# Order of weight and conditioning loads, unbroken conditioning visits and a run of ten output products in a hybrid decoder block

## The chip, the core and the metric

The kernel runs on one core of one Trainium2 chip. The metric is the device time of one execution in microseconds (us). The kernel before takes 1383.16 us, the median of three runs (1382.48 to 1385.14).

A core has five engines that run their own instruction streams: TensorE (PE) does matrix products, with the loads of its stationary operand listed apart as PEld; VectorE (DVE), ScalarE (ACT) and GpSimd (POOL) work on elements; SyncE (SP) issues DMAs here. Sixteen DMA engines move data between main memory and the core. Each engine takes its instructions in the order of its own stream, so an instruction that waits holds up all that stands behind it on that engine.

## What is computed

One layer of a decoder for two groups of tokens: 256 tokens of a prompt and 8 x 4 tokens of samples, 288 columns in all, with a model width of 2048. Cut to what matters:

```python
mod = silu(c) @ w_ada + b_ada                 # 6 parts of 2048 per conditioning vector
sh1, sc1, g1, sh2, sc2, g2 = split(mod, 6)
h = rmsnorm(x, norm1) * (1 + sc1) + sh1
u_pool, z, xbc, dt_raw = split(h @ w_in)      # 512, 1536, 2560, 24 columns
pool_out = pool_mixer(u_pool)
ssd_out  = ssd_mixer(z, xbc, dt_raw)          # conv, 24 heads x 64, state 128, chunks of 128
x = x + g1 * (concat(pool_out, ssd_out) @ w_out)
h2 = rmsnorm(x, norm2) * (1 + sc2) + sh2
gate, val = split(h2 @ w_up)                  # 2 x 5504
x = x + g2 * ((silu(causal_conv(gate)) * val) @ w_down)
y = rmsnorm(x, norm_f)
```

All is float32. `c` has nine rows: one for the prompt, eight for the samples. "Conditioning" below means the product of silu(c) with the 2048 x 12288 matrix `w_ada`.

## The kernel before, in words

**Layout.** Activations lie with features on the 128 partitions and the 288 tokens along the free axis; the width of 2048 is 16 feature tiles (KT). A large product is done as three matmuls in a reduced float32 format (`mm3`, L224 to L228): the weight tile is split into a high part (a cast on ScalarE, L220) and a low part (a subtraction on VectorE, L221), the activation likewise (h1h, h1l; L368, L369), and high x high, high x low and low x high are summed in PSUM. Each weight comes from main memory in loads of 512 KB (`load`, L210 to L213), issued by the sync queue in the order of its stream, into a ring of "raw" slots: 16 during the first stage, 8 after it, 9 from the output projection on.

**Order.** The code is written as generators that yield after a unit of work, and `pull(gen, rate)` (L871) runs another generator by so many units. What is written earlier has the higher priority; a planner then fills each engine's stream, taking of the instructions that its model holds to be ready the one with the highest priority. `tc.high_priority()` raises an instruction above the rest, and `tc.keep_in_program_order` keeps it behind the instruction written last on that engine. The order on each engine is fixed when the program is built.

**First stage.** The input projection cannot start before the first norm is modulated, and the modulation needs two parts (shift and scale) of the conditioning. Both are therefore cut by feature tiles into six groups, `KGROUPS`, of 1, 1, 2, 4, 4 and 4 tiles. `ada_group_units(gi)` (L275) loads the `w_ada` columns of a group (4, 4, 8, 16, 16, 16 loads), multiplies them in visits of four loads (records "adag", L303), transposes the result ("adat_g"), and `modulate` (L352) makes h1h and h1l of the group. `xbc_units(gi)` (L554) then multiplies the group's rows of `w_in` for 28 column tiles (a unit is one column tile; in groups 0 and 1 one load holds eight units) and adds the result to what the groups before gave: group 0 is copied from PSUM by ScalarE (L574), the others are added by VectorE (L576). The generator `nxt` runs the conditioning of groups 1 to 5 and their modulation. Its first five units come ahead of the products of group 0, and during group `gi` it is pulled at `AN[gi+1] / (ET - 4)` per unit, with ET = 28.

**Second stage.** With group 5 come the convolution, the state space mixer (`ssd_group`, L634), the pooling mixer and the remaining columns of `w_in` (records "mm_uz"), all interleaved (`back`). In `ssd_group`, `decays(t)` makes for two heads the decay factors e (all tokens) and ec (second chunk), with the last step of both on VectorE; `outputs(t)` (L725) sums ten products of 64 columns for the two heads into one PSUM bank: yo with a selection matrix, and xdt of each chunk with e, and s1 (the state after the first chunk) with ec. Each float32 product appears as two records in the trace.

**Later conditioning.** Four further parts of the conditioning are not needed at once. `ada_part_units(part, ay)` (L329) goes through the 16 feature tiles: two loads and four products each with 32 output rows in a column strip of their own (`ada_mm`, L252; records "adap", L255). Parts 2, 3 and 4 run with AY = 2, so a unit, or "visit", is two feature tiles: four loads, eight products, 16 records. They are pulled a fraction of a visit at a time during the second stage and the output projection (`adas`). Part 5 runs with `ay` = 1 during the first pairs of the gated MLP.

**Then** follow the output projection ("mm_out"), the up projection in pairs of gate and value ("mm_gate", "mm_val"), interleaved with the down projection in three groups ("mm_down"), and the last norm.

Of the kernel before, what the change touches and what calls it, by code (L numbers as in the profile page):

```python
# [17 lines left out]
P = 128  # L18
D = 2048
KT = D // P  # L20
NP = 256
NB, NL = 8, 4
NS = NB * NL
N = NP + NS
# [11 lines left out]
ET = XT + len(UEARLY) + 3 * ZEARLY  # L36
# [4 lines left out]
YK = 2  # L41
AQ = (4, 4, 4, 4, 4, 4)

AN = (5, 5, 7, 11, 14, 15)
AY = 2

RA1, RA2, RB1, RB2, RB3 = 0.5, 0.4, 1.0, 1.0, 1.0
# [86 lines left out]
def kernel(ctx: ExitStack, tc, ins, outs):  # L134
    nc = tc.nc
# [8 lines left out]
    def aux(name):  # L144
        return px.tile([P, 512], F32, tag="aux", name=name)
# [11 lines left out]
    seli = vec[:, K_SEL:K_SEL + 32]  # L157
# [9 lines left out]
    sc_c = kp.tile([P, KT, 32], F32, name="sc_c")  # L167
# [42 lines left out]
    def load(key):  # L210
        off, cols = S.items[key]
        t = wp[0].tile([P, RAWC], F32, tag="raw", name="raw_" + "_".join(map(str, key)))
        nc.sync.dma_start(t[:, :cols], wflat[off:off + P * cols].rearrange("(p n) -> p n", p=P))  # L213
        return t

    def split(raw, a, n, name, urgent=True):
        hi = wp[0].tile([P, RAWC], F32R, tag="whi", name="whi_" + name)
        lo = wp[0].tile([P, RAWC], F32R, tag="wlo", name="wlo_" + name)
        with tc.high_priority() if urgent else nullcontext():
            nc.scalar.copy(hi[:, :n], raw[:, a:a + n])  # L220
            nc.vector.tensor_tensor(lo[:, :n], raw[:, a:a + n], hi[:, :n].bitcast(F32), ALU.subtract)  # L221
        return hi, lo

    def mm3(ps, whi, wlo, c, bh, bl, first, last, n=P):  # L224
        w = slice(c * n, c * n + n)
        nc.tensor.matmul(ps, whi[:, w], bh, start=first, stop=False)  # L226
        nc.tensor.matmul(ps, whi[:, w], bl, start=False, stop=False)  # L227
        nc.tensor.matmul(ps, wlo[:, w], bh, start=False, stop=last)  # L228

    ready = {}  # L230
# [21 lines left out]
    def ada_mm(ps, raw, k, c0, nb, js):  # L252
        for j in js:
            c = c0 + (j - js[0]) * nb
            nc.tensor.matmul(ps[32 * j:32 * j + 32, :nb], sc_c[:, k, :], raw[:, c:c + nb],  # L255
                             start=(k == 0), stop=(k == KT - 1), tile_position=(0, 32 * j))

    def ada_sb(ps, nb, name, r=P):
        asb = kp.tile([P, 512], F32, tag="asb", name="asb_" + name)
        nc.scalar.copy(asb[0:r, :nb], ps[0:r, :nb])  # L260
        return asb

    def ada_tr(asb, nb, name, r=P):
        pt = aux("adat_" + name)
        for i in range(nb // P):
            nc.tensor.transpose(pt[:, i * r:(i + 1) * r], asb[0:r, i * P:(i + 1) * P], ident[0:r, 0:r])
        return pt

    def ada_scale(which, part, norm, k0, gk):
        nc.vector.scalar_tensor_tensor(  # L270
            out=amul[:, which, k0:k0 + gk, :], in0=ada[:, part, k0:k0 + gk, :], scalar=1.0,
            in1=norm[:, k0:k0 + gk].unsqueeze(2).to_broadcast([P, gk, NC9]),
            op0=ALU.add, op1=ALU.mult)
# [54 lines left out]

    def ada_part_units(part, ay=1):  # L329
        ps = pa.tile([P, 512], F32, tag="ada", name=f"adap{part}")  # L330
        for k in range(KT):
            raws = [load(("adap", part, k, h)) for h in range(2)]
            for h in range(2):
                ada_mm(ps, raws[h], k, 0, 512, range(2 * h, 2 * h + 2))
            if k % ay == ay - 1:
                yield
        asb = ada_sb(ps, 512, f"p{part}")
        yield
        pt = ada_tr(asb, 512, f"p{part}")
        for i in range(4):  # L340
            o = ada[:, part].rearrange("p (j i) c -> p j i c", j=4)[:, :, i, :]
            b = bada[:, part].rearrange("p (j i) -> p j i", j=4)[:, :, i]
            src = pt[:, i * P:(i + 1) * P].rearrange("p (j c) -> p j c", j=4)[:, :, 0:NC9]
            nc.vector.tensor_tensor(o, src, b.unsqueeze(2).to_broadcast([P, 4, NC9]), ALU.add)
        if part == 4:
            ada_scale(1, 4, vec[:, V_N2:V_N2 + KT], 0, KT)
        yield
# [56 lines left out]
    for q in range(4):  # L404
        t = mx.tile([P, 4, N], F32, tag="blk", name=f"xa{q}", bufs=4)
# [11 lines left out]
    for q in range(4):  # L417
# [216 lines left out]
    def ssd_group(g):  # L634
# [10 lines left out]
        xdt = kp.tile([P, 3, G6], F32, tag="hmod", name=f"xdt{g}", bufs=2)  # L645
# [27 lines left out]
        s1 = sx[0].tile([P, G6], F32, tag="s1", name=f"s1_{g}")  # L673
# [18 lines left out]
        for i in range(2):  # L692
            for j in range(4):
# [3 lines left out]
                                 tile_position=(0, 32 * j))  # L697
        yo = sx[0].tile([P, G6], F32, tag="yo", name=f"yo{g}")
# [26 lines left out]
        def outputs(t, e, ec):  # L725
            assert (g, t) in zdone
            pq = aux(f"y{g}_{t}")
            rows = [slice(0, 64), slice(64, P)]
            for i, r in enumerate(rows):
                f = slice(64 * (2 * t + i), 64 * (2 * t + i) + 64)  # L730
                nc.tensor.matmul(pq[r, NP:N], yo[:, f], seli, start=True, stop=False)
            for i, r in enumerate(rows):
                f = slice(64 * (2 * t + i), 64 * (2 * t + i) + 64)
                nc.tensor.matmul(pq[r, NP:N], xdt[:, 2, f], e[:, i, NP:N], start=False, stop=True)
            for i, r in enumerate(rows):
                f = slice(64 * (2 * t + i), 64 * (2 * t + i) + 64)
                nc.tensor.matmul(pq[r, 0:P], xdt[:, 0, f], e[:, i, 0:P], start=True, stop=True)
            for i, r in enumerate(rows):
                f = slice(64 * (2 * t + i), 64 * (2 * t + i) + 64)
                nc.tensor.matmul(pq[r, P:NP], xdt[:, 1, f], e[:, i, P:NP], start=True, stop=False)  # L740
                nc.tensor.matmul(pq[r, P:NP], s1[:, f], ec[:, i, :], start=False, stop=True)
            yt = cf[:, t, 0:N]
            nc.vector.scalar_tensor_tensor(out=yt, in0=yt,
                                           scalar=vec[:, V_D + 3 * g + t:V_D + 3 * g + t + 1],
                                           in1=pq[:, :N], op0=ALU.mult, op1=ALU.add)
            zt = zy[g][:, t, :]
            nc.vector.tensor_tensor(zt, zt, yt, ALU.mult)
            sq = kp.tile([P, N], F32, tag="xsq", name=f"ysq{g}_{t}", bufs=2)
            nc.scalar.activation(sq, zt, AF.Square)
            if g + t == 0:  # L750
                nc.gpsimd.tensor_copy(ssq, sq)
            else:
                nc.gpsimd.tensor_tensor(ssq, ssq, sq, ALU.add)
# [117 lines left out]
    def pull(gn, rate):  # L871

        credit[id(gn)] = credit.get(id(gn), 0.0) + rate
        while credit[id(gn)] >= 1:
            credit[id(gn)] -= 1
            next(gn, None)

    ready["xbc", 0, 0] = load(("xbc", 0, 0))
    for _ in range(AN[0]):
        next(nxt)  # L880
    for gi in range(len(KGROUPS)):
        last = gi + 1 == len(KGROUPS)
        if last:

            wp[0].drop(w0)
            w0_ctx.close()
            sx[0] = mx_ctx.enter_context(tc.tile_pool(name="sx", bufs=1, reuse_waits="tile"))
            hi, lo = split(load(("dt",)), 0, KT * NH, "dt")
            ps = pm.tile([P, 512], F32, tag="mm", name="mm_dt")
            for k in range(KT):  # L890
                mm3(ps[0:NH, :N], hi, lo, k, xhi[0][k], xlo[0][k], k == 0, k == KT - 1, NH)
            late_states()
            dt_stage(ps)
        elif gi == 1:
            nc.sync.dma_start(vec, ins["vec"])
        elif gi == 4:
            late_loads()
        for i, m in enumerate(xbc_units(gi)):
            if not last:
                pull(nxt, AN[gi + 1] / (ET - 4))  # L900
                if i == ET - 4 and gi == 4:
                    drain(nxt)
            else:
                pull(back, 0.5 if m < 20 else RB1) if m >= 9 else None
                pull(adas, RA1 / AY)
# [34 lines left out]
    for g in range(4):  # L940
        for t in range(3):
            k = 4 + 3 * g + t
# [352 lines left out]
```

## Time and profile before

| | before |
|---|---|
| median of three runs | 1383.16 us |
| the profiled execution | 1382.64 us |
| its span, first to last instruction | 1380.9 us |
| mean granted TensorE clock | 0.993 |
| TensorE busy | 1357.1 us, 98% |
| VectorE busy | 822.1 us, 60% |
| ScalarE busy | 575.8 us, 42% |
| GpSimd busy | 222.8 us, 16% |
| read from main memory | 309.78 MB |

How to read it: the span is from the first to the last instruction of the profiled execution. A matmul's busy time includes its way through the array, which overlaps with the next one, so an engine that reads 98% busy need not be at its peak rate. Rows in order of time give the start, the busy time, the engine, the line of the kernel, the operation, "out<-in" by the program's names, the shape, and the number of instructions merged into the row; in brackets the idle time ahead of it and what ended it. Rows by stretch give for each engine the busy time and the number of instructions, then the granted clock of TensorE, the share of the DMA engines and the rate.

### The profile page before, as it was taken

To read this page: it belongs to the slowest core of one execution; us is meant where nothing else is said; L and a number is where in the kernel's file an instruction comes from. 1 tells how busy PE (TensorE), PEld (TensorE's weight loads), DVE (VectorE), ACT (ScalarE), POOL (GpSimd) and SP (SyncE) were. 2 spreads that over 40 slices of the span, in tenths; PEclk is the share of its full clock that TensorE was granted. 3 is DMA by queue.
4 is the path that set the end of the run, shared out by engine and by line. 5 is a ranking of instruction groups with operands and counts; after the bars stand their busy time and mean duration, and the time that the engine had idled before them with its cause. 6 is when DMAs were issued, how large, how long until landed. Compare 5 with 4: busy or idle time off the path is not lost.

```text
span 1380.9 us, 26414 instructions
## 1 busy us (share of the span) xinstructions
PE 1357.1 (98%) x10557; PEld 1256.4 (91%) x10557; DVE 822.1 (60%) x1450; ACT 575.8 (42%) x925; POOL 222.8 (16%) x426
## 2 busy tenths in 40 slices
PE   7899999999999999999999999999999999999997
PEld 6789887776679898998999999999999999999997
DVE  3686667977674448655655545665555556565553
ACT  3432334378653334533443333444343333443452
POOL 0000001222222123111211001222120012122221
PEclk9999999999999999999999999999999999999998
DMA  9997876888788877788655555655555555665531
GB/s 373 357 341 287 309 261 255 316 297 298 271 330 320 323 277 254 234 275 290 205 179 180 166 169 184 202 191 186 182 181 161 177 193 188 198 187 193 187 119 69
DMA packets 97194, 323.20 MB, mean 234 GB/s; under 512 B 10736, under 2 KB 19888, under 8 KB 97072
## 3 DMA queue, kind: packets, MB, share of 16 engines
q1 hardware_dynamic: 93168, 310.63, 65.2%
q0 software_dynamic: 3184, 9.69, 1.9%
q8 instruction: 83, 1.36, 0.4%
q10 hardware_dynamic: 720, 1.19, 0.2%
q14 instruction: 39, 0.32, 0.1%
HBM read 309.78 MB, written 10.39 MB: 232 GB/s over the span
## 4 chain that ended last, share of the span: by engine, by line
PE 94%; DVE 3%; DMA 1%; ACT 1%; issue 1%; POOL 0%; SPq 0%; DVEq 0%; ACTq 0%; POOLq 0%
PE mm_down L226 7%; PE mm_down L228 7%; PE mm_down L227 7%; PE mm_gate L228 6%; PE mm_gate L226 6%; PE mm_val L227 6%; PE mm_gate L227 6%; PE mm_val L228 6%; PE mm_val L226 6%; PE adap L255 4%; PE xbc L226 4%; PE xbc L228 4%; PE xbc L227 4%; PE mm_out L226 3%; PE mm_out L227 2%; PE mm_out L228 2%
## 5 line engine op out<-in xcount | busy, mean ns | idle before, releaser
L226 PE MATMUL mm_down<-ah,whi_down 128*128 128x288 f32 x688 | 203.7, 296 | 0.0
L228 PE MATMUL mm_down<-ah,wlo_down 128*128 128x288 f32 x688 | 203.5, 296 | 0.0
L227 PE MATMUL mm_down<-al,whi_down 128*128 128x288 f32 x688 | 203.3, 295 | 0.0
L228 PE MATMUL mm_gate<-h2h,wlo_gate 128*128 128x288 f32 x640 | 190.2, 297 | 0.0
L226 PE MATMUL mm_gate<-h2h,whi_gate 128*128 128x288 f32 x640 | 189.8, 297 | 0.0
L227 PE MATMUL mm_gate<-h2l,whi_gate 128*128 128x288 f32 x640 | 189.3, 296 | 0.0
L227 PE MATMUL mm_val<-h2l,whi_val 128*128 128x288 f32 x640 | 188.8, 295 | 0.0
L228 PE MATMUL mm_val<-h2h,wlo_val 128*128 128x288 f32 x640 | 188.5, 295 | 0.0
L226 PE MATMUL mm_val<-h2h,whi_val 128*128 128x288 f32 x640 | 188.0, 294 | 0.0
L221 DVE TENSOR_TENSOR wlo_gate<-raw_gate,whi_gate 128x1024 fp32r<-128x1024 f32 x80 | 97.9, 1225 | 139.4 <-ACT whi_gate L220 139.3
L221 DVE TENSOR_TENSOR wlo_down<-raw_down,whi_down 128x1024 fp32r<-128x1024 f32 x96 | 107.8, 1123 | 117.0 <-ACT whi_down L220 116.1
L220 ACT CAST whi_down<-raw_down 128x1024 fp32r<-128x1024 f32 x96 | 92.2, 961 | 168.6 <-PE mm_down L227 120.6
L220 ACT CAST whi_gate<-raw_gate 128x1024 fp32r<-128x1024 f32 x80 | 83.9, 1050 | 163.7 <-PE mm_gate L227 75.4
L226 PE MATMUL xbc<-h1h,whi_xbc 128*128 128x288 f32 x448 | 137.0, 307 | 6.9 <-ACT whi_xbc L220 3.4
L220 ACT CAST whi_val<-raw_val 128x1024 fp32r<-128x1024 f32 x80 | 84.1, 1051 | 123.3 <-issue 104.2
L227 PE MATMUL xbc<-h1l,whi_xbc 128*128 128x288 f32 x448 | 133.4, 298 | 0.4 <-DVE h1l L369 0.4
L228 PE MATMUL xbc<-h1h,wlo_xbc 128*128 128x288 f32 x448 | 132.4, 300 | 1.2 <-DVE wlo_xbc L221 0.9
L227 PEld LDWEIGHTS mm_down<-al,whi_down 128*128 128x128 f32 x688 | 129.7, 189 | 0.0
L228 PEld LDWEIGHTS mm_down<-ah,wlo_down 128*128 128x128 f32 x688 | 129.6, 188 | 0.0
L226 PEld LDWEIGHTS mm_down<-ah,whi_down 128*128 128x128 f32 x688 | 129.6, 188 | 0.0
L226 PEld LDWEIGHTS mm_gate<-h2h,whi_gate 128*128 128x128 f32 x640 | 120.4, 188 | 5.0 <-ACT ah L1060 3.4
L227 PEld LDWEIGHTS mm_gate<-h2l,whi_gate 128*128 128x128 f32 x640 | 120.7, 189 | 0.0
(318 smaller groups left out, 2994.4 us busy)
## 6 DMA issues: line engine op xcount, KB each, us to landing
raw_adap<-wflat SPq DMA_DIRECT2D x128, 512.0 KB, 6.0
raw_gate<-wflat SPq DMA_DIRECT2D x80, 512.0 KB, 3.6
raw_val<-wflat SPq DMA_DIRECT2D x80, 512.0 KB, 3.6
raw_ada<-wflat SPq DMA_DIRECT2D x64, 512.0 KB, 8.3
raw_xbc<-wflat SPq DMA_DIRECT2D x55, 512.0 KB, 6.8
raw_down<-wflat SPq DMA_DIRECT2D x48, 512.0 KB, 3.6
raw_out<-wflat SPq DMA_DIRECT2D x32, 512.0 KB, 7.8
raw_down<-wflat SPq DMA_DIRECT2D x32, 384.0 KB, 3.1
```

Of the source, the lines that this page charges most:

```text
L220: nc.scalar.copy(hi[:, :n], raw[:, a:a + n])
L221: nc.vector.tensor_tensor(lo[:, :n], raw[:, a:a + n], hi[:, :n].bitcast(F32), ALU.subtract)
L226: nc.tensor.matmul(ps, whi[:, w], bh, start=first, stop=False)
L227: nc.tensor.matmul(ps, whi[:, w], bl, start=False, stop=False)
L228: nc.tensor.matmul(ps, wlo[:, w], bh, start=False, stop=last)
L255: nc.tensor.matmul(ps[32 * j:32 * j + 32, :nb], sc_c[:, k, :], raw[:, c:c + nb], start=(k == 0), stop=(k == KT - 1), tile_position=(0, 32 ...
```

## The change

Three things are changed.

- In the first stage the first two weight loads of group 0, instead of one, are issued ahead of the conditioning of group 1. The pull rates of `nxt` are new, and a table AT gives the unit of a group from which it is pulled: in group 0 only from the tenth unit on.
- In `ada_part_units` a visit first issues all its loads and then does its products in reversed order of the loads. All products but the first are raised in priority and kept in the order in which they are written, so that once the first is placed the others follow it.
- In `outputs` the ten products are written as one list: xdt of the second chunk with e, s1 with ec, xdt of the first chunk with e, xdt of the samples with e, and yo last, each for both heads. All but the first are raised in priority and kept in that order.

```diff
-AN = (5, 5, 7, 11, 14, 15)
+AN = (5, 4, 9, 12, 16, 15)
+AT = (10, 0, 0, 0, 0)
 AY = 2
...
     def ada_part_units(part, ay=1):
         ps = pa.tile([P, 512], F32, tag="ada", name=f"adap{part}")
-        for k in range(KT):
-            raws = [load(("adap", part, k, h)) for h in range(2)]
-            for h in range(2):
-                ada_mm(ps, raws[h], k, 0, 512, range(2 * h, 2 * h + 2))
-            if k % ay == ay - 1:
-                yield
+        for ka in range(0, KT, ay):
+            raws = [(k, h, load(("adap", part, k, h))) for k in range(ka, ka + ay) for h in range(2)]
+
+            begun = False
+            for k, h, raw in raws[::-1]:
+                for j in (2 * h, 2 * h + 1):
+                    with tc.high_priority() if begun else nullcontext():
+                        i = nc.tensor.matmul(ps[32 * j:32 * j + 32, :512], sc_c[:, k, :],
+                                             raw[:, (j % 2) * 512:(j % 2) * 512 + 512],
+                                             start=(k == ay - 1), stop=(k == KT - ay), tile_position=(0, 32 * j))
+                    if begun:
+                        tc.keep_in_program_order(i)
+                    begun = True
+            yield
...
             rows = [slice(0, 64), slice(64, P)]
-            for i, r in enumerate(rows):
-                f = slice(64 * (2 * t + i), 64 * (2 * t + i) + 64)
-                nc.tensor.matmul(pq[r, NP:N], yo[:, f], seli, start=True, stop=False)
...
+            fs = [slice(64 * (2 * t + i), 64 * (2 * t + i) + 64) for i in range(2)]
+
+            prods = [(P, NP, lambda i: (xdt[:, 1, fs[i]], e[:, i, P:NP]), True, False),
+                     (P, NP, lambda i: (s1[:, fs[i]], ec[:, i, :]), False, True),
+                     (0, P, lambda i: (xdt[:, 0, fs[i]], e[:, i, 0:P]), True, True),
+                     (NP, N, lambda i: (xdt[:, 2, fs[i]], e[:, i, NP:N]), True, False),
+                     (NP, N, lambda i: (yo[:, fs[i]], seli), False, True)]
+            begun = False
+            for n0, n1, ops, first, last in prods:
+                for i, r in enumerate(rows):
+                    with tc.high_priority() if begun else nullcontext():
+                        ins = nc.tensor.matmul(pq[r, n0:n1], *ops(i), start=first, stop=last)
+                    if begun:
+                        tc.keep_in_program_order(ins)
+                    begun = True
...
-    ready["xbc", 0, 0] = load(("xbc", 0, 0))
+    for ci in range(2):
+        ready["xbc", 0, ci] = load(("xbc", 0, ci))
     for _ in range(AN[0]):
         next(nxt)
...
             if not last:
-                pull(nxt, AN[gi + 1] / (ET - 4))
+                if i >= AT[gi]:
+                    pull(nxt, AN[gi + 1] / (ET - 4 - AT[gi]))
```

More of the change, by code (lines that the diff above doesn't have):

```diff
@@ L728, in outputs @@
             rows = [slice(0, 64), slice(64, P)]
-            for i, r in enumerate(rows):
-                f = slice(64 * (2 * t + i), 64 * (2 * t + i) + 64)
[L731 to L741, printed above, removed]
+            fs = [slice(64 * (2 * t + i), 64 * (2 * t + i) + 64) for i in range(2)]
[12 more added lines that the diff above has]
+                    begun = True
             yt = cf[:, t, 0:N]
```

## The prediction

> **What bounds the kernel now.** I read the page first, then busy time by stage, then TensorE's and ScalarE's instructions in order of time in the stages that the change touches.
>
> ```profile
> PE 1357.1 (98%) x10557; PEld 1256.4 (91%) x10557; DVE 822.1 (60%) x1450; ACT 575.8 (42%) x925; POOL 222.8 (16%) x426
> PE 94%; DVE 3%; DMA 1%; ACT 1%; issue 1%; POOL 0%; SPq 0%; DVEq 0%; ACTq 0%; POOLq 0%
> ```
>
> TensorE bounds the kernel: 98% busy and 94% of the chain that ended last. So time comes from three things only: gaps in front of a matmul, slices at a lower clock, and TensorE time that computes nothing. The next view (busy time of each engine by stretch; the first number behind the comma is PE busy, then PEld, DVE, ACT, POOL, granted clock, DMA share, GB/s) shows the first two.
>
> ```profile
> 27.38:30.80 3.42, 0.60 (x10) 0.30 (x2) 1.32 (x5) 1.33 (x3) 0.64 (x2) 1.00 1.03 407
> 30.80:37.63 6.83, 6.13 (x22) 5.44 (x23) 2.38 (x2) 2.92 (x13) 0.00 (x0) 0.50 1.03 407
> 61.52:97.00 35.48, 35.48 (x322) 31.35 (x325) 29.91 (x91) 10.82 (x14) 0.83 (x2) 1.00 0.92 351
> 235.00:280.00 45.00, 44.80 (x330) 32.98 (x329) 38.85 (x89) 21.36 (x32) 10.48 (x17) 1.00 0.81 291
> 280.00:400.00 120.00, 117.43 (x953) 84.15 (x950) 85.36 (x156) 89.13 (x199) 28.37 (x37) 1.00 0.80 294
> ```
>
> From 27.38 TensorE works 0.60 us in 3.42, and for the next 6.83 us its clock is 0.50. From 61.52 to 97 it is never without work, so what is gained ahead of that is kept. From 235 to 400 it is busy 162 of 165 us, but VectorE is at 86% up to 280: second in line.
>
> **Part 1: weights ahead of conditioning, first feature group.** Why is TensorE idle at 28? In order of time, TensorE, then ScalarE, then the DMA issues of the sync queue:
>
> ```profile
> 31.17 0.61 PE L226 MATMUL xbc<-h1h,whi_xbc 128*128 128x288 f32 x1 [2.75 <-ACT whi_xbc L220]
> 46.31 0.40 PE L226 MATMUL xbc<-h1h,whi_xbc 128*128 128x288 f32 x1 [0.65 <-ACT whi_xbc L220]
> ...
> 29.73 0.43 ACT L368 CAST h1h<-h_g 128x288 fp32r<-128x288 f32 x1 [1.80 <-POOL h_g L366]
> 30.07 1.04 ACT L220 CAST whi_xbc<-raw_xbc 128x1024 fp32r<-128x1024 f32 x1
> ...
> 15.77 0.33 SPq L213 DMA_DIRECT2D raw_xbc<-wflat  x1
> 27.01 0.33 SPq L213 DMA_DIRECT2D raw_xbc<-wflat  x1
> ...
> raw_xbc<-wflat SPq DMA_DIRECT2D x1, 512.0 KB, 11.2
> ```
>
> The last row is the landing time of the load issued at 15.77: the second weight chunk lands at 15.77 + 11.2 = 27.0. It is cast only at 30.07, because ScalarE takes the cast of the next group's activations (h1h) first and stands 1.80 us before it. So TensorE waits 2.75 us, and the half clock follows that stretch. The change loads this chunk second, ahead of the four conditioning loads; at one load per 1.3 us (an estimate: 512 KB at the 407 GB/s above), and with six conditioning loads behind it instead of ahead, it lands near 19. TensorE then goes from chunk one to chunk two without the wait, and group 1's conditioning runs beside 24 ready matmuls. No DMA is added: the conditioning loads come one place, 1.3 us, later.
>
> What is gained is when group 1's own weights start, at 46.31. What ends last before that is ScalarE. Its work from 21 to 47:
>
> ```profile
> L574 ACT COPY cvp<-xbc 128x256 f32<-128x256 f32 (+1 forms) x40 | 8.6, 294 | 7.0 <-PE xbc L228 7.0
> L220 ACT CAST whi_xbc<-raw_xbc 128x1024 fp32r<-128x1024 f32 (+1 forms) x4 | 3.8, 946 | 0.0
> ```
>
> ScalarE stands 7.0 us waiting for TensorE there. The part of it ahead of the very first copy stays; I take 5.5, because the 1.80 us ahead of h1h remain too, but now with TensorE at work beside them. Cross-check: the gap 2.75 plus half of the 6.83 us at half clock (3.4) is 6.2. Ends: 7.7 (all 7.0 and the gap of 0.65 ahead of 46.31) and -1.3 (conditioning late by one load and nothing else). The first weight load of group 1, issued at 27.01, keeps its place among the loads, so it does not limit a start at 41. **-5.5 us.**
>
> The new rates (9, 12, 16 pulls for 7, 11, 14, the first ten units of group 0 without one) bring the conditioning of groups 3 to 5 some six to eight units earlier. TensorE has no gap at those borders now, so I cost this at nothing; the cover is the same busy TensorE, and without it a late modulation would show as a gap like the 2.75 above. The price, loads of conditioning ahead of weights, is hidden while DMA stands at 0.92.
>
> [...]
>
> **Part 2: unbroken visits.** A visit of the later conditioning is four loads and 16 matmul records (AY = 2). Whole, then in pieces:
>
> ```profile
> 218.58 1.92 PE L255 MATMUL adap<-raw_adap,sc_c 128*32 128x512 f32 x16
> 220.67 0.29 PE L227 MATMUL xbc<-h1l,whi_xbc 128*128 128x288 f32 x1
> ...
> 197.49 1.05 PE L255 MATMUL adap<-raw_adap,sc_c 128*32 128x512 f32 x2
> 198.70 0.29 PE L227 MATMUL xbc<-h1l,whi_xbc 128*128 128x288 f32 x1
> 198.83 0.29 PE L226 MATMUL xbc<-h1h,whi_xbc 128*128 128x288 f32 x1
> 199.19 1.07 PE L255 MATMUL adap<-raw_adap,sc_c 128*32 128x512 f32 x8
> 285.26 1.90 PE L255 MATMUL adap<-raw_adap,sc_c 128*32 128x512 f32 x10
> 288.06 1.06 PE L255 MATMUL adap<-raw_adap,sc_c 128*32 128x512 f32 x6
> 353.06 1.04 PE L255 MATMUL adap<-raw_adap,sc_c 128*32 128x512 f32 x2
> ```
>
> From its start to the second ordinary matmul behind it the whole visit takes 220.67 - 218.58 = 2.09, the two-record piece 198.70 - 197.49 = 1.21. By their busy times two, six and eight records cost 1.04 to 1.07, ten and sixteen 1.90 and 1.92: what counts is the number of pieces. The visit at 197 is three pieces of two, eight and six: 3 x 1.21 - 2.09 = 1.54 more than whole. Ten and six cost 1.90 + 1.06 - 1.92 = 1.04 more, less 0.1 of overlap at the end of a piece. Of the 24 visits of parts 2 to 4 most are whole already. Ahead of 390 six are cut: at 197 into three, at 285 into two, at 353 into three (the first one shown), and in the same way (no row quoted) at 235, 312 and 321 into two: 1.54, 2 x 0.95 at 353, and 4 x 0.95: 7.2 us. Two more cut visits lie where TensorE waits anyway, near 400 and 522; I count nothing for them, up to 1.5 us at best.
>
> What it costs. All four loads now have to be there before the first matmul, and in reversed order the slot loaded first, which the queue needs back first, comes free last: about 0.9 us later, half of a visit. Where that matters, the chain of the end shows:
>
> ```profile
> SPq L213 <- PE adap L255: 119.6, 38, 8.0
> 247.49 1.07 PE adap L255 x8
> 248.94 6.92 DMA raw_xbc<-wflat
> 255.96 1.05 ACT whi_xbc L220
> ```
>
> The sync queue waits 119.6 us, in 38 waits, for slots that such visits hold; at 247.5 half a visit frees the slot that a weight load needs, and it is cast as it lands. Twice 0.9 there, with a little lost to the loaded VectorE: of 7.2 I keep 5. Ends: 9 (with the two late visits) and -20 (every visit loses 0.9, the fifth case). **-5 us.** The part 5 visits (one step of two loads) gain nothing: they run in pairs as one piece. VectorE covers the rest up to 280, with 14% to spare.
>
> **Part 3: ten products in one run.**
>
> ```profile
> 289.51 0.31 PE L731 MATMUL y<-vec,yo 128*64 128x32 f32 x4
> 289.75 0.41 PE L226 MATMUL mm_uz<-h1h,whi_uz 128*128 128x288 f32 x1
> 290.21 0.31 PE L734 MATMUL y<-e,xdt 128*64 128x32 f32 x4
> 291.18 0.40 PE L228 MATMUL mm_uz<-h1h,wlo_uz 128*128 128x288 f32 x1
> ...
> 372.68 0.31 PE L731 MATMUL y<-vec,yo 128*64 128x32 f32 x4
> 373.77 0.40 PE L226 MATMUL mm_uz<-h1h,whi_uz 128*128 128x288 f32 x1
> ```
>
> Now the two products with yo start as soon as yo is there, and the other eight when the decays are: 289.51 to 289.75 and 290.21 to 291.18, 1.21 us in two pieces, against 372.68 to 373.77, 1.09, in the one block that is whole. The break itself costs more: 0.70 us pass from 289.51 to 290.21 for 0.24 of products and two ordinary matmuls, which elsewhere start 0.13 apart (198.70 to 198.83), so 0.2 goes into leaving and entering again. Together 1.21 + 0.2 - 1.09 = 0.32. In the 12 blocks of the four head groups 11 are cut: 3.5 us. The new order starts with the products of e, and the third needs ec, which VectorE makes just behind e. Where ec is late, the run is cut after the second product as it is now after the yo pair, or TensorE stands for it. The fp32 products themselves are the same. Ends: 3.5 and -2 (a short stand in each block); I take 2.5, nearest to the whole block. **-2.5 us.**
>
> **Sum.** 5.5 + 5 + 2.5 = 13 us off the profiled execution's own 1382.64: 1369.6. The median of the runs, 1383.16, lies 0.5 above that execution, so I say 1370. 0.2% is 2.8 us.
>
> **Rivals.**
> (1) The sum: 1370; own range 1362 to 1376: the upper ends 7.7 + 9 + 3.5 give 1362.4 and half of each term 1376. Chance 0.56.
> (2) TensorE time saved from 235 to 400 turns into waits for VectorE (86% busy there). Only part 1 and the visit at 197 (1.5) stay: 7 us, 1375.5. For it: 2.6 us of gaps in 280 to 400. Against it: TensorE has loose work there, the uz products. Chance 0.14.
> (3) The gap moves instead of going: ScalarE stands before h1h while chunk three waits, and the clock drops there. Parts 2 and 3 alone: 1375. Chance 0.11.
> [...] Chance 0.05.
> (5) Slower: slots that come free 0.9 us late. 24 visits at 0.9 are 21 us, against 13 gained: 1391. It decides from 15 visits on whose next weight load is on the path; now the chain shows one such stretch, though 38 waits of the queue stand for it. Chance 0.09.
> (6) No change: each part meets a wait of its own size (ScalarE's order, a slot, a late ec), 1382. Chance 0.05.
>
> Range: 1362 to 1380 holds cases 1 to 4 with their ends; it leaves out 5, 6 and a little more. Faster: 0.56 + 0.14 + 0.11 + 0.05 = 0.86; same 0.05; slower 0.09.
>
> **What would show it.** Part 1: no wait of 2.75 before an xbc matmul near 28, clock 1.00 up to 38, first group-1 matmul near 41 in place of 46.3. Part 2: 16 records in each adap piece. Part 3: y pieces of 20 records. Wrong it would be if adap pieces stay cut, if the queue's waits for adap grow and casts of xbc or out stand before TensorE, or if a new half-clock stretch appears ahead of 60.

## The result: slower, and the profile after

The changed kernel takes 1386.4 us, the median of 20 runs (1382.42 to 1391.41), against 1382.69 us of the kernel before on the same chips (1380.59 to 1385.14, 20 runs). The ratio is 1.0028, with a 95% interval of 1.0020 to 1.0036: 3.9 us slower, where 13 us faster were predicted. The profiled execution took 1388.28 us, 1.9 us above that median; its span is 1386.5 us.

The page of the changed kernel, TensorE's share of busy time and the engines' shares of the chain that ended last:

```profile
PE 1350.8 (97%) x10557; PEld 1259.3 (91%) x10557; DVE 825.5 (60%) x1450; ACT 577.4 (42%) x925; POOL 226.7 (16%) x426
PE 88%; DVE 6%; DMA 3%; ACT 1%; issue 1%; POOL 0%; SPq 0%; DVEq 0%; ACTq 0%; POOLq 0%
```

TensorE has 6.3 us less to do (1357.1 before) while the span is 5.6 us longer. So about 12 us of new standing took more than the edits saved. In the chain TensorE falls from 94% to 88%; VectorE and the DMA take over, 3% to 6% and 1% to 3%. Where? The busy time by stretch, with the columns of the prediction:

```profile
29.73:33.15 3.42, 2.67 (x63) 2.15 (x51) 0.76 (x3) 1.20 (x5) 0.43 (x2) 1.00 1.04 408
33.15:36.56 3.41, 1.06 (x6) 0.83 (x6) 2.67 (x3) 1.38 (x2) 0.21 (x1) 1.00 1.02 405
36.56:43.39 6.83, 6.42 (x46) 5.70 (x50) 1.28 (x4) 3.80 (x15) 0.00 (x0) 0.50 1.02 408
61.52:97.00 35.48, 32.70 (x299) 26.68 (x297) 28.34 (x86) 9.67 (x13) 0.86 (x2) 1.00 0.87 314
235.00:280.00 45.00, 44.49 (x332) 35.81 (x334) 40.12 (x99) 20.29 (x30) 8.01 (x15) 1.00 0.90 339
280.00:400.00 120.00, 114.27 (x988) 87.06 (x984) 86.25 (x157) 88.22 (x194) 30.06 (x41) 0.99 0.79 293
```

The stretch with little work and the half clock behind it have not gone. They have moved by 6 us: 1.06 us of work from 33.15 to 36.56, then 6.83 us at clock 0.50. From 61.52 to 97, where TensorE was busy throughout, it now works 32.70 of 35.48 us. From 280 to 400 it works 114.27 us of 120, 3.2 less than before.

ScalarE, and then TensorE, in order of time at the new gap:

```profile
31.32 0.27 ACT L261 COPY asb_g<-adag 128x128 f32<-128x128 f32 x1 [1.64 <-PE adag L304]
...
33.39 0.43 ACT L377 CAST h1h<-h_g 128x288 fp32r<-128x288 f32 x1 [0.49 <-POOL h_g L375]
33.73 1.04 ACT L221 CAST whi_xbc<-raw_xbc 128x1024 fp32r<-128x1024 f32 x1
```

```profile
34.82 0.40 PE L227 MATMUL xbc<-h1h,whi_xbc 128*128 128x288 f32 x1 [2.42 <-ACT whi_xbc L221]
36.90 0.61 PE L229 MATMUL xbc<-h1h,wlo_xbc 128*128 128x288 f32 x1 [1.02 <-DVE wlo_xbc L222]
```

This is the picture of before, one weight chunk later. The third chunk, issued at 16.71, landed at 28.42 by the records of its transfer. ScalarE casts it only at 33.73, because in its stream the cast of the next group's activations (h1h) stands ahead, and h1h waits for the whole conditioning of group 1. Chunk two now comes early, and the same wait stands before chunk three.

The waits of TensorE from 20 to 110, one row of after and one of before (us in total, times, longest):

```profile
PE xbc L229 <- DVE wlo_xbc L222: 4.0, 7, 1.0
```

```profile
PE xbc L228 <- DVE wlo_xbc L221: 0.9, 2, 0.6
```

Behind the gap TensorE now waits for freshly split weights 4.0 us instead of 0.9. The first addition of a group starts in the two traces so (us, from the records of the additions; the two experiments in the last columns, both run on the kernel before, are told of below):

| group | before | after | rates alone (e6) | cast first (e9) |
|---|---|---|---|---|
| 1 | 48.02 | 49.48 | 45.46 | 43.32 |
| 2 | 71.15 | 75.86 | 71.82 | 65.75 |
| 3 | 101.34 | 107.35 | 103.34 | 96.04 |
| 4 | 154.97 | 162.08 | 158.06 | 149.66 |
| 5 | 214.43 | 219.10 | 215.09 | 209.12 |

Each column is one execution. Six of the experiments below leave the first stage as it was; in their traces and that of before TensorE has the same order up to 196 us, and the first addition of group 4 still lies between 153.53 (e1) and 157.15 (e15). So a row that differs by less than 3.6 us shows nothing by itself.

Parts 2 and 3 did what they say. From 180 to 386 us all 16 visits are whole in the trace of after, and of the twelve runs of ten eleven are whole (20 records). The chain shows what follows some visits (start, us, what):

```profile
223.32 1.92 PE adap L339 x16
225.72 6.70 DMA raw_xbc<-wflat
232.55 0.91 issue
234.14 1.21 DVE wlo_xbc L222
...
292.72 1.01 PE y L749 x20
...
315.94 1.93 PE adap L339 x16
317.89 6.65 DMA raw_uz<-wflat
324.62 1.04 ACT whi_uz L221
```

Twice a visit ends, a weight load of 6.7 us starts, and its cast or subtraction follows as it lands: the slot that the load needs came free with the visit. The chain of before had one such place in this stretch (247 to 256).

### The profile page after: what moved, and what is told of

It reads as the page before. It is cut to its first block, busy times and chain, and to the rows that moved or that the text cites. A ratio compares the mean times of both kernels' runs of the same rounds, so it can differ in the third digit from the quotient of the medians.

```text
span 1386.5 us, 26395 instructions
## 1 busy us (share of the span) xinstructions
PE 1350.8 (97%) x10557; PEld 1259.3 (91%) x10557; DVE 825.5 (60%) x1450; ACT 577.4 (42%) x925; POOL 226.7 (16%) x426
## 4 chain that ended last, share of the span: by engine, by line
PE 88%; DVE 6%; DMA 3%; ACT 1%; issue 1%; POOL 0%; SPq 0%; DVEq 0%; ACTq 0%; POOLq 0%
PE mm_down L229 7%; PE mm_down L227 7%; PE mm_down L228 7%; PE mm_gate L229 6%; PE mm_gate L227 6%; PE mm_val L228 6%; PE mm_gate L228 6%; PE mm_val L229 6%; PE mm_val L227 6%; PE xbc L227 4%; PE xbc L229 4%; PE xbc L228 4%; PE adap L339 3%; PE mm_out L227 3%; PE mm_out L228 3%; PE mm_out L229 2%
```

## The experiments

All times are medians; the ratio is to the kernel before, run beside it on the same chip (1382.8 us there), and the last column is that ratio times 1382.8.

| | kernel | us | ratio, 95% interval | against before, us |
|---|---|---|---|---|
| | the whole change | 1386.40 | 1.0028, 1.0020 to 1.0036 | +3.9 |
| e1 | visits alone | 1380.73 | 0.9991, 0.9982 to 1.0001 | -1.2 |
| e2 | run of ten alone | 1379.43 | 0.9973, 0.9962 to 0.9984 | -3.7 |
| e3 | first stage alone | 1386.67 | 1.0026, 1.0016 to 1.0035 | +3.6 |
| e4 | visits and run | 1381.48 | 0.9983, 0.9975 to 0.9992 | -2.4 |
| e5 | second chunk ahead, old rates | 1380.15 | 0.9978, 0.9969 to 0.9987 | -3.0 |
| e6 | new rates, no second chunk | 1383.17 | 0.9999, 0.9990 to 1.0007 | -0.1 |
| e9 | e5, cast ahead of h1h | 1376.74 | 0.9954, 0.9941 to 0.9966 | -6.4 |
| e10 | e4, no visit ahead of the output projection | 1381.80 | 0.9989, 0.9978 to 0.9999 | -1.5 |
| e11 | e9 and run | 1373.16 | 0.9934, 0.9921 to 0.9947 | -9.1 |
| e12 | e9, run and visits | 1378.40 | 0.9968, 0.9956 to 0.9980 | -4.4 |
| e13 | e9 with the new rates | 1379.81 | 0.9978, 0.9969 to 0.9988 | -3.0 |
| e14 | before, mixer not normed | 1380.25 | 0.9986, 0.9978 to 0.9995 | -1.9 |
| e15 | e4, mixer not normed | 1375.78 | 0.9953, 0.9939 to 0.9967 | -6.5 |
| e16 | e11 with nine slots | 1378.41 | 0.9962, 0.9950 to 0.9975 | -5.3 |
| e17 | e12 with nine slots | 1368.84 | 0.9894, 0.9880 to 0.9907 | -14.7 |

### Which part loses? e1 to e4

Each kernel has the diff of the change for its part and the code of before for the rest. Theory A puts the loss in the first stage, its rival B in the visits.

> The kernel before with the unbroken visits alone. Theory A (the loss of the whole change sits in the first stage, the visits give TensorE time back and lose a part of it where they were filling waits): 1 to 4 us faster than before, all adap pieces of 16 records (8 at the ends of part 5), with longer waits near 400 and 530. Theory B (the loss sits in the visits, through slots that come free late and filler that is gone): 2 to 5 us slower, with waits of TensorE for casts of xbc or out.

> The kernel before with the ten products in one run alone. Theory A: y pieces of 20 records, 0 to 2 us faster, since short waits for e take back part of the 3.5 us of TensorE time. Theory B: the waits for e outweigh, 1 to 3 us slower.

> The kernel before with the first-stage edits alone (two weight loads ahead, new rates). Theory A: 4 to 8 us slower, a wait of 2 to 3 us near 32 for the cast of the third weight chunk that stands behind h1h, half clock behind it, the first group-1 add later than before. Theory B: within 2 us of before.

> The change without its first-stage edits. Theory A: 2 to 5 us faster than before, and so 6 us or more below the whole change. Theory B: slower than before, about as the whole change.

The first stage alone is 3.6 us slower, as slow as the whole change: theory A. The visits lose nothing, but bring 1.2 us with an interval that touches zero, and the run of ten brings 3.7, more than either theory said. Together these two bring 2.4, less than the run by itself. So two things are to be explained: a first stage that loses, and visits that bring next to nothing.

### The first stage: e5, e6, e9, e13

e5 has the second chunk ahead with the old rates, e6 the new rates without it:

```diff
 # e5
-    ready["xbc", 0, 0] = load(("xbc", 0, 0))
+    for ci in range(2):
+        ready["xbc", 0, ci] = load(("xbc", 0, ci))
 # e6
-AN = (5, 5, 7, 11, 14, 15)
+AN = (5, 4, 9, 12, 16, 15)
+AT = (10, 0, 0, 0, 0)
```

> The kernel before with the second weight load of group 0 ahead of the conditioning of group 1, and the old pull rates. Theory C (the new rates cost the time, since they put conditioning loads ahead of weight loads while the DMA engines have no slack): within 1.5 us of before; the wait of 2.75 us near 28 moves to the third weight chunk, near 32, and the half clock with it. Theory D (the preload costs the time, since the gap that it moves is followed by more waits): 3 to 4 us slower, like the first-stage edits together.

> The kernel before with the new pull rates alone (and no pull in the first ten units), without the preload. Theory C: 3 to 5 us slower, with waits of TensorE for the low part of xbc weights between 55 and 105. Theory D: within 1 us of before.

Alone, the load brings 3.0 us and the rates nothing; together they cost 3.6. Neither theory had that: e6's time is the one that theory D gave, but D's cause, a load that costs, is refuted by e5. The traces tell why they don't add. First e5, then e3, TensorE in order of time:

```profile
31.68 1.95 PE L303 MATMUL adag<-raw_ada,sc_c 128*32 128x128 f32 x64
34.44 0.40 PE L226 MATMUL xbc<-h1h,whi_xbc 128*128 128x288 f32 x1 [0.81 <-ACT whi_xbc L220]
```

```profile
30.58 0.29 PE L229 MATMUL xbc<-h1h,wlo_xbc 128*128 128x288 f32 x1
33.30 0.40 PE L227 MATMUL xbc<-h1h,whi_xbc 128*128 128x288 f32 x1 [2.44 <-ACT whi_xbc L221]
```

With the old rates the first conditioning visit of group 2 falls into the wait for chunk three and covers it but for 0.81 us. With the table AT the pulls begin only at the tenth unit and that visit comes at 40.44 in e3, so nothing covers the wait: 2.44 us, with a half clock of 6.83 us behind it. In e6 the longest gap from 24 to 40 is 0.64 us: there ScalarE casts chunk two at 28.42, ahead of h1h at 31.20. Its first group-1 addition comes at 45.46, 2.6 us ahead of before; by group 2 that is gone (71.82 against 71.15), and by group 3 it is 2 us behind.

If ScalarE's order makes the gap, putting chunk three's cast ahead of h1h must remove it. e9 takes group 1's products and modulation behind that chunk, and keeps the copy of its conditioning (asb_g) in the written order:

```diff
 # e9, on e5
-AN = (5, 5, 7, 11, 14, 15)
+AN = (4, 5, 7, 11, 14, 15)
...
-        nc.scalar.copy(asb[0:r, :nb], ps[0:r, :nb])
+        i = nc.scalar.copy(asb[0:r, :nb], ps[0:r, :nb])
+        if pin:
+            tc.keep_in_program_order(i)
...
-                pull(nxt, AN[gi + 1] / (ET - 4))
+                if gi == 0:
+                    if i == 16:
+                        next(nxt)
+                    elif i > 16:
+                        pull(nxt, 0.53)
+                else:
+                    pull(nxt, AN[gi + 1] / (ET - 4))
```

> As e5_preload, but with the products and the modulation of group 1 written behind the third weight chunk of group 0, and ScalarE's copy of group 1's conditioning pinned there, so that the cast of the third chunk stands ahead of h1h. If ScalarE's order makes the gap: no wait above 1 us between 22 and 40, clock 1.00 up to 40 at least, and the first group-1 add 3 us or more earlier than before; 2 to 6 us faster than before. If the gap is set by landing loads or by the conditioning chain itself: it stays in another place and the time is within 1.5 us of before.

It takes 1376.74 us, 6.4 less than before, a little more than the 2 to 6 that were expected. ScalarE, and the stretch from 22 to 40:

```profile
29.96 1.06 ACT L220 CAST whi_xbc<-raw_xbc 128x1024 fp32r<-128x1024 f32 x1
...
35.30 0.43 ACT L370 CAST h1h<-h_g 128x288 fp32r<-128x288 f32 x1 [0.33 <-POOL h_g L368]
```

```profile
22.00:40.00 18.00, 17.22 (x211) 15.89 (x211) 6.26 (x11) 12.96 (x53) 0.64 (x2) 0.91 1.03 407
```

The cast comes at 29.96 and h1h 5 us behind it. TensorE is busy 17.22 of 18 us, with no wait above 0.5 us. The granted clock is 0.91 and not the 1.00 that was expected: one stretch of 3.41 us at half clock starts at 21.73. With the cast ahead of h1h the gap is gone. The edit isn't that order alone, though: it also brings chunk three's load forward, from issue at 19.77 and landing at 29.99 in e5 to 13.97 and 25.60. An early landing is not what the gap hangs on in the changed kernel, where chunk three had been there for 5.3 us when it was cast (28.42 and 33.73); and a chunk that lands at 29.99 would still be about in time for a cast at 29.96. No run has the one without the other. The sum that I made for part 1, 5.5 us, is near what this buys (6.4); the load alone doesn't buy it.

e13 puts the new rates on top, 9, 12 and 16 for 7, 11 and 14:

> The cast of chunk three ahead of h1h (1376.7 us), with the new rates 9, 12, 16 from group 1 on. If the new rates cost time of their own (weight loads late behind conditioning, as the milestones of the kernel with the rates alone say: about 3 us in group 1, 1 each in groups 2 and 3, of which 2 come back in group 4): 2 to 4 us slower than without them, 1379 to 1381. If their cost was only that they let the gap and the half clock return: 1376 to 1377.

It takes 1379.81 us. That is 3.4 us slower than e9 by the ratios, as the first theory had it, with no gap to return. The rates themselves cost. TensorE's waits for split weights from 40 to 155, in e9 and in e13:

```profile
PE xbc L228 <- DVE wlo_xbc L221: 0.5, 2, 0.3
```

```profile
PE xbc L228 <- DVE wlo_xbc L221: 2.5, 6, 0.6
```

Weights do land later: the 12th load of xbc weights at 66.5 us in e13 and at 62.7 in e9, the 23rd at 105.7 and 99.1. The two traces don't show the whole 3.4 us. The first addition of group 5 comes at 209.70 in e13, only 0.6 us behind e9, though e9 had one stretch of 3.41 us at half clock more by then. 1.6 us more are lost between there and the end; where, isn't shown.

The run times fit two terms, read from the same runs: the gap and what follows it at about 3 us, the rates at about 3.4. e5 takes most of the gap away (-3.0); e6 takes it away and pays the rates (-0.1); e3 pays the rates and keeps the gap (+3.6). How the 3 us divide is open: in e5's trace half clock still takes 10.24 us ahead of 60, in three stretches of 3.41, as much as in before (6.83 and 3.41).

### The visits: e10, e14, e15

In e4 the visits and the run had gained 5.3 us by the first product of the output projection (391.79 against 397.05), of which 1.0 was left at the end of the span. The stretches of e4 where it goes (three, of 3.41 us or twice that):

```profile
378.61:382.02 3.41, 3.41 (x16) 3.41 (x16) 1.98 (x3) 2.18 (x5) 0.66 (x1) 0.50 0.95 346
392.27:395.68 3.41, 0.00 (x0) 0.00 (x0) 3.41 (x13) 3.41 (x10) 1.89 (x2) 1.00 0.89 276
395.68:402.51 6.83, 5.39 (x21) 2.13 (x22) 2.48 (x8) 0.26 (x1) 0.00 (x0) 0.50 1.01 369
```

TensorE stands a whole 3.41 us between mixer and output projection, and runs 6.83 us at half clock behind it. It waited 4.93 us there for the fourth load of an unbroken visit:

```profile
397.12 3.64 PE L338 MATMUL adap<-raw_adap,sc_c 128*32 128x512 f32 x16 [4.93 <-DMA raw_adap<-wflat]
```

e10 keeps visits out of that place:

```diff
-TA, ADA_OUT = 4, 4
+TA, ADA_OUT = 0, 4
```

> Visits and run of ten as in e4_visits_run, but with no visit pulled between the mixer and the output projection (TA = 0), where a visit there stood 4.9 us for its fourth load. If the visit's wait for all four loads is what takes the gain back: the wait and the half clock near 395 go, 2 to 5 us faster than e4_visits_run. If TensorE would wait there for the mixer's output anyway: the wait is named mixl or pout instead, and the time is that of e4_visits_run within 1 us.

1381.8 against 1381.5 us: no difference. The stand stays, 4.80 us from 387.86, and is now one for the normed mixer output (mixl):

```profile
392.66 0.61 PE L227 MATMUL mm_out<-mixl,whi_out 128*128 128x288 f32 x1 [4.80 <-DVE mixl L955]
```

So the visit's loads are not what makes this place late. e14 and e15 leave the four multiplications of the norm out of that chain, one on the kernel before, one on e4; their output differs for it:

```diff
         for g in range(4):
-            (nc.gpsimd if g == 3 else nc.vector).tensor_tensor(zy[g], zy[g],
-                                    (rstdy if g else rstdyp).unsqueeze(1).to_broadcast([P, 3, N]), ALU.mult)
             yield
```

> Before, without the four multiplications that scale the mixer's output by its norm (three on VectorE, one on GpSimd); the output differs for that. It is the base for the next kernel. The mixer tiles of head groups 0 to 2 can then be cast as soon as their y is there, so the stands of before between 388 and 400 should go: 1 to 4 us faster than before, 1379 to 1382.

> Unbroken visits and the run of ten, again without those four multiplications. Theory: the visits gain 4 to 5 us up to 390 and the wait for VectorE's chain (y, norm, mix) between the mixer and the output projection takes it back, with the half clock behind it. Without the norm's step that chain is short: 6 to 9 us less than the base without the norm, no stand over 2 us between 380 and 400. Rival: the gain is lost elsewhere (slots that come free late, the conditioning's own loads): 1 to 3 us less than that base, as with the norm (1381.5 against 1382.8).

By the ratios the two parts bring 4.6 us here instead of 2.4, between the two expectations. From the first addition of group 5 to the end, which leaves the first stage out, the traces say 6.0 (1163.7 against 1157.8 us). The same stretch without this edit gives 1.2 (1166.5 against 1165.3 us). So the place between mixer and output projection seems to take a part of the gain, but the 2.2 us by the ratios have an uncertainty of some 2.5, and the traces are one execution each. It isn't all: in e15 TensorE still waits 4.3 us for the decay factor e between 205 and 400.

### The visits on a mended first stage: e11, e12, and nine slots, e16, e17

e11 is e9 with the run of ten, e12 is e11 with the unbroken visits.

> The first stage as in the kernel that put the cast of chunk three ahead of h1h (6.3 us under before), with the run of ten products (3.7 under before alone). If the two touch different stages and neither lands on the other's wait: 6.0 + 3.7 = 9.7 under before, 1373 us. Rival: a saving ahead of 390 ends in the wait for the last y and mix tiles, as it did where the visits and the run were joined (1.2 and 3.7 alone gave 2.3): then 1376 to 1377, and a stand of over 2 us with a half clock behind it near 385 to 395.

> The same with the unbroken visits as well, so all three parts of the change, with the old rates and the cast of chunk three ahead of h1h. If the visits are worth their 4 to 5 us once the first stage is mended: 1368 to 1369. If the wait for VectorE and ScalarE between the mixer and the output projection takes them, as in the joined kernel of visits and run: 1373 to 1376, no better than without the visits, with TensorE standing 4 to 5 us near 385 to 392 and a half clock of 6.83 behind it.

e11 takes 1373.16 us, as the sum of the two says. e12 is 4.7 us slower than e11 by the ratios, worse than both expectations. Its waits of TensorE from 205 to 400, and the longest of those for e:

```profile
PE y L750 <- DVE e L731: 6.0, 4, 2.5
PE adap L340 <- DMA raw_adap<-wflat: 4.0, 1, 4.0
```

```profile
376.45 0.44 PE L750 MATMUL y<-e,xdt 128*64 128x128 f32 x4 [2.52 <-DVE e L731]
```

What made e late is on ScalarE and in the sync queue's issues:

```profile
372.83 1.04 ACT L220 CAST whi_uz<-raw_uz 128x1024 fp32r<-128x1024 f32 x1 [3.17 <-DMA raw_uz<-wflat]
373.78 0.68 ACT L730 ACTIVATE e<-e 128x576 f32<-128x576 f32 x1
```

```profile
358.54 7.40 SPq L213 DMA_DIRECT2D raw_adap<-wflat  x4
366.05 1.69 SPq L213 DMA_DIRECT2D raw_uz<-wflat  x2
367.83 7.65 SPq L213 DMA_DIRECT2D raw_adap<-wflat  x4
```

Read from below: the last of four visit loads stands in the sync queue for a slot until 365.61, and the uz weight behind it is issued at 366.05. It lands at 372.75. ScalarE stands 3.17 us for it, because the cast of a weight is raised in priority and was put ahead of the exponential of e; the exponential ends at 374.46, VectorE's product follows at 375.05, behind the low part of the same weight, and TensorE has stood 2.52 us. No decay and no y depends on that weight. They only stand behind it on ScalarE (3.17 us) and on VectorE, where the low part takes 1.23 us from 373.90.

If slots are the cause, one more must give the gain back. e16 and e17 are e11 and e12 with nine weight slots in the second stage:

```diff
-RAW0, RAW1, RAW2 = 8, 8, 1
+RAW0, RAW1, RAW2 = 7, 9, 0
...
-        ncv = sx[0].tile([P, 5, 27], F32, tag="ncv", name=f"ncv{g}")
+        ncv = sx[0].tile([P, 5, 27], F32, tag="pools", name=f"ncv{g}", bufs=2)
...
-        s2 = sx[0].tile([P, G6], F32, tag="s2", name=f"s2_{g}")
+        s2 = sx[0].tile([P, G6], F32, tag="bt", name=f"s2_{g}")
```

> The first stage with the cast ahead of h1h and the run of ten (1373.2 us), with nine weight slots instead of eight in the second stage (s2 shares the buffer of bt, ncv that of the pooling's scratch tiles; seven instead of nine slots are added for the first stage). The base for the next kernel. The queue then waits less for slots that visits hold (67 us in 21 waits between 205 and 400 with eight): 0 to 3 us faster, 1370 to 1373.

> The same with unbroken visits as well. With eight slots the visits cost 5.2 us here (1378.4 against 1373.2). Theory S: a visit that waits for all four loads and gives the first slot back last keeps the queue standing, the next weight lands late, ScalarE stands for it, and the decay factor e behind it comes late (2.5 us ahead of one block of y). A ninth slot takes most of that away: at most 1 us slower than the nine-slot base, perhaps 1 to 3 faster, and less than 3 us of waits for e between 280 and 380 (6.0 with eight). Rival V: VectorE's and ScalarE's own work sets the time there, and the slots are not the cause: still 4 to 6 us slower than the base, waits for e as with eight slots.

The same visits that cost 4.7 us with eight slots gain 9.4 with nine. Of the 9.4, 3.8 make up for what the ninth slot alone costs (e16 against e11); slot and visits together bring 5.5 over e11. e17 takes 1368.84 us, ratio 0.9894 (0.9880 to 0.9907), the best of all. Two waits of e17 in the same stretch:

```profile
PE mm_out L227 <- DVE mixl L964: 0.5, 1, 0.5
PE y L750 <- DVE e L731: 0.5, 1, 0.5
```

The waits for e fall from 6.0 to 0.5 us, and TensorE no longer waits for a visit's load. This was theory S, and its effect is larger than it said. The base e16 missed its expectation by 5 us: with the ninth slot and without the unbroken visits the kernel is 3.8 us slower than e11. Its visits are cut more often. Two that are whole in e11 (from 326 to 341 of its trace), and the same two in e16:

```profile
329.09 1.92 PE L255 MATMUL adap<-raw_adap,sc_c 128*32 128x512 f32 x16
338.37 1.92 PE L255 MATMUL adap<-raw_adap,sc_c 128*32 128x512 f32 x16
```

```profile
323.43 1.05 PE L255 MATMUL adap<-raw_adap,sc_c 128*32 128x512 f32 x2
327.14 1.92 PE L255 MATMUL adap<-raw_adap,sc_c 128*32 128x512 f32 x14
...
333.41 1.04 PE L255 MATMUL adap<-raw_adap,sc_c 128*32 128x512 f32 x2
336.19 1.07 PE L255 MATMUL adap<-raw_adap,sc_c 128*32 128x512 f32 x8
338.20 1.06 PE L255 MATMUL adap<-raw_adap,sc_c 128*32 128x512 f32 x6
```

From 180 to 386 the 256 records of the visits form 24 pieces in before and in e11, 29 in e16, and 16 in e12. Five more at 0.95 us are 4.8 us, more than the 3.8 that e16 loses; that is worked out and not tested by a run of its own. A rival is not tested either: to make room, e16 and e17 let s2 and ncv share buffers with other tiles; what that alone costs no run shows. Nor was the ninth slot tried without the mended first stage.

## Why the prediction was wrong, point by point

**Part 1, "-5.5 us".** This is the step that failed, together with the rates below. The two measured +3.6 (e3), 9 us off. I took it that with chunk two ahead "TensorE then goes from chunk one to chunk two without the wait, and group 1's conditioning runs beside 24 ready matmuls". It did, and 24 matmuls at 0.13 us (an estimate from the starts at 198.70 and 198.83) are 3.1 us, while the h1h ahead of chunk three's cast came 5 us after that chunk had landed (33.39 and 28.42). I had seen that ScalarE takes h1h first and never asked where the next chunk's cast stands in the same order; the third rival did, at a chance of 0.11. The load alone brought 3.0 (e5), because the next conditioning visit covered the wait for chunk three; the ten units without a pull, part of the same edit, took that cover away, and the gap moved. That 5.5 is near the 6.4 of e9 is no check of the sum: e5 takes all but 0.81 us of the gap and brings half of it.

**"The new rates ... I cost this at nothing; the cover is the same busy TensorE."** They cost 3.4 us (e13 against e9). I had read the busy TensorE as cover. It was the one to be fed: conditioning loads come ahead of weight loads in one queue, and from 43 to 66 us the DMA engines are full in e13, as they are in e9 (a share of 1.03 in both), so more conditioning there means weights that land later (by 3.8 us for the 12th). The stretch of e13, the DMA share in the column before the last:

```profile
43.00:66.00 23.00, 20.06 (x216) 15.57 (x215) 19.28 (x61) 4.69 (x7) 0.77 (x2) 1.00 1.03 408
```

The 0.92 that I relied on is the mean of the stretch behind that. The later waits account for some 2 of the 3.4 us; the rest is open.

**Part 2, "-5 us".** By itself the edit brought 1.2 us (interval 0 to 2.5). The saving of TensorE time was right by the count of pieces: 8 fewer at 0.95 us, the estimate from the rows of part 2, are 7.6, where I had counted 7.2. What ate it is, by the runs on the mended first stage, the mechanism of the fifth case, slots that come free late, at a size between my "twice 0.9" and its 21 us: the same edit is worth -9.4 us with nine slots and +4.7 with eight on the mended first stage. I priced a late slot by the weight's own products. The price came by another way: the late weight's cast stands on ScalarE, and the decay factors stand behind it (6.0 us of waits for e in e12, 0.5 in e17). "Against it: TensorE has loose work there, the uz products" fails for the same reason, since the uz products are what waits for that weight. Rival 2 named the place (280 to 400) and the wait (VectorE), but its cause, VectorE's load of work, was not it: e17 has the same work on VectorE and waits 0.5 us for e, where e12 waits 6.0.

**"Two more cut visits ... I count nothing for them."** One of them turned into a stand of 3.6 us in e1 and 4.93 in e4, there with 6.83 us at half clock from 395.68, where I had allowed only for a gain. With that visit moved away (e10) the time stayed, so by itself it isn't what took the gain.

**Part 3, "-2.5 us".** Right in its mechanism. The runs say 3.7 (e2), and 2.7 as the difference of e11 and e9 by the ratios; my upper end was 3.5. In the trace of after the blocks are runs of 20 records but for one cut after four (the 16 at 346.40 in its chain), so a late ec did cut once and cost little: one ordinary matmul stands between, from 346.00 to 346.33.

**The half clock and the gap.** Part 1's cross-check counted the half clock with the gap, and in these traces the two go together. In the nine traces with a gap of 2.4 us or more from 28 to 35 us a stretch of 6.83 us at half clock comes with it; in the eight where no gap there is over 0.81 us, none has such a stretch. In e9 two of 3.41 us are left (from 21.73 and from 52.45).

**The sum.** The parts measured alone give +3.6 and -2.4, 1.2 us slower; the change measured 3.9. The rest, 2.7 with an uncertainty of about 2, is not settled. In the trace of after a half clock of 3.41 us comes twice between 391 and 409, where before has none.

## What to carry to other kernels

When a wait goes from the path, look up the next instruction of its kind in the same engine's stream and ask what that one stands behind: in the changed kernel chunk three had landed at 28.42 and was cast at 33.73, so an earlier load alone would not have brought that cast forward. In e12 one late load was passed on to work that has nothing to do with it (3.17 us on ScalarE, then 2.52 of TensorE's wait for e), so a price for late buffers has to be read from what is queued behind the waiting instruction. An edit that makes a step hold its buffers longer should be tried with one buffer more before it is judged; here that turned a loss of 4.7 us into a gain of 9.4, or of 5.5 for the buffer and the edit together.

## What the runs showed of the hardware that was not expected

In the traces of before and after, up to the end of the work, the stretches at half clock last 3.41 us or 6.83, twice that, and the stretches at full clock between them whole multiples of it too (20.48 in before, 10.24 in after; 27.31 in e9); their position differs from one execution to the next (the one of 6.83 us starts at 30.80 in before, at 30.45 in e4). So in these traces the clock changes in steps of 3.41 us. e4 and e15 have the same instruction order on TensorE for the first two thousand matmul records, and both have the gap of 2.75 us (at 30.90 and 32.11). Yet the clock drops once more in e15. Two stretches of 3.41 us of e4, and two of e15:

```profile
20.21:23.62 3.41, 2.22 (x12) 1.77 (x13) 2.48 (x5) 1.45 (x7) 0.00 (x0) 1.00 1.02 406
23.62:27.03 3.41, 3.41 (x78) 3.23 (x76) 0.00 (x0) 2.26 (x12) 0.00 (x0) 1.00 1.03 411
```

```profile
19.40:22.81 3.41, 1.80 (x10) 1.26 (x9) 2.96 (x6) 0.98 (x5) 0.00 (x0) 1.00 1.03 411
22.81:26.22 3.41, 3.40 (x14) 3.41 (x15) 0.00 (x0) 2.20 (x11) 0.00 (x0) 0.50 1.03 412
```

In e4 the stretch around the small gaps of the start held 2.22 us of work and the clock stayed; in e15 it lay 0.8 us earlier (0.5 as measured from the first xbc matmul), held 1.80, and the next stretch ran at half clock. The first addition of group 2 comes at 73.35 in e15 and at 70.86 in e4. So a single profile of this kernel can be off by 2 us and more with nothing changed ahead of the place that is read, and differences of that size were judged here by repeated runs. The gap of 2.75 us is shorter than such a stretch, and 6.83 us at half clock came with it all the same (from 30.45 in e4, from 33.05 in e15). The work in one stretch does not tell the clock of the next by itself: in e10 one with 1.58 us (from 56.20) was followed by full clock, in e17 one with 2.23 (from 373.02) by half.
